# A matrix product by fast multiplication on one core: quarter sums moved between engines, sums of x ahead of weighings, one memory pool per buffer

## The chip, the cores and the metric

The kernel runs on one core of one Trainium2 chip. The metric is device time in microseconds (us), the median of several runs. TensorE (PE) multiplies, VectorE (DVE) and ScalarE (ACT) do element-wise work, GpSimd (POOL) does a little of it, and SyncE (SP) issues nearly all the DMAs. Each engine works through its own queue in order, and waits on semaphores for the others.

## The reference

```python
B, S, D = 8, 2048, 2048          # x: (B, S, D), w: (D, D), float32
cs = np.cumsum(x, axis=1)
diff = cs - np.concatenate([zeros, cs[:, :-1, :]], axis=1)
return np.matmul(diff, w)
```

The difference of a cumulative sum is x itself, so what has to be computed is x @ w: 16384 x 2048 times 2048 x 2048. The kernel does not build the sum.

## The kernel before

**Tiles.** The 16384 rows of x are 128 tiles of 128 rows. Tiles 0 to 3 (`PLAIN = 4`) are multiplied plainly in bf16 while w is still coming in. The other tiles are taken in groups of four, `g, g+1, g+2, g+3`, in float16. A group is two pairs of tiles, (g, g+1) and (h, h+1) with h = g + 2, and each pair is multiplied with w by a scheme of Strassen and Winograd's kind: x and w are split into 2 x 2 blocks, sums and differences of blocks are formed (`S1` to `S4` of x, `T1` to `T4` of w), seven block products are taken instead of eight, and the results are added up. From the second group on some of the seven products are themselves split so, with quarter blocks: `Inner` holds the quarter sums of one block of w (`Q1` to `Q4`, made by `first`, `third` and `fourth`), `sums_in` makes those of x (`one` and `two`, for different blocks `one4`, `two4`, and so on). The first group, `group_plain`, uses block products alone; the second, at g = 8, takes the branch of `group` where `five` is false; the third and all later ones take the other branch.

**One tile of x** goes through these steps: `load` (two DMAs of 512 KB into a buffer of `F`, on SP's queue), `weigh` (ScalarE sums absolute values, half a row at a time), `scale_of` (VectorE makes the row's scale of it, GpSimd the unit `u` with which results are scaled back), `narrow` (ScalarE scales and casts to float16), `turn` (two DMA transposes on SP's queue). `where[t]` says which two buffers of `F` tile t uses: tile 7 (`PLAIN + 3`) uses `F[:, 2]` and `F[:, 3]`. Tile 5 is loaded into the room of `xP`, the plain tiles' x.

**Results** are gathered in float32 tiles `c` of 128 x 512: `keep` copies a PSUM bank into one (ScalarE), `add` adds a bank to it (VectorE), `put` stores it (SP's queue). `keeps`, `adds` and `puts` do this for two.

**Order.** The order on every engine is written by hand. Each instruction goes through a helper that ties it behind the last one of its engine:

```python
def after(engine, ask):
    if engine in last:
        with tc.issue_after(last[engine].ins):
            said = ask()
    ...
```

So the place of a line in the source is its place in that engine's queue. A line of the profile is that of the helper: L515 is the matmul of `product`, L534 that of `quarter`, L545 `add`, L542 `keep`, L505 `total` (sums of x), L502 `less` (differences of w), L357 and L361 `block` (w scaled to float16, by VectorE and ScalarE), L425 the making of `T1`, L112 `weigh`, L129, L131 and L132 `scale_of`, L143 `narrow`, L156 `turn`, L100 `load`, L556 `put`, L260 the store of a plain result, L250 the plain matmul.

**The head** is all up to the first group. When the plain tiles of the second half of w are done (`finish_row`), eight results `done` are stored from tiles of the pools `ring` and `o`, and `left_over` makes the one plain block that had no room. Then those pools are closed and their memory is used by the pools of `c` (`cpool`, on `ring`) and of `inner` (`inpool`, on `o` and on `first`, which holds `xP`). `inner` holds in its parts `S1` of both pairs, the sums in passing (`passing`), quarter sums of w, and in the first group two results. A tile that takes memory of a closed pool waits for the last use of what lay there.

In the first group VectorE's queue between the product of `S1g` and that of `S2h` reads as follows; in the second group GpSimd makes one set of quarter differences:

```python
scale_of(h + 1)                    # first group, h + 1 = 7
less(T2[6:], B22[6:], T1[6:])
...
total(S4g, A12g, S2g, SUB)
less(T3, B22, B12)
scale_of(g + 4)
total(S1h, A21h, A22h, ADD); total(S3h, A11h, A21h, SUB); total(S2h, S1h, A11h, SUB)
```
```python
in_4.first()                       # second group: Q1 and Q2, eight differences on DVE
in_4.third("pool")                 # four on GpSimd
```

Of the kernel before, what the change touches and what calls it, by code (L numbers as in the profile page):

```python
# [10 lines left out]
def kernel(  # L11
# [6 lines left out]
    nc = tc.nc  # L18
    P = 128
# [5 lines left out]
    KH = KO // 2  # L25
    NH = N // 2
# [49 lines left out]
# [4 lines that stand above are left out]
        else:  # L80
            said = ask()
        last[engine] = said[-1] if isinstance(said, tuple) else said
        return said
# [74 lines left out]
                    ),  # L158
                )

    with tc.tile_pool(name="ring", bufs=7) as ring, tc.tile_pool(
        name="o", bufs=5
    ) as opool, tc.tile_pool(name="first", bufs=1) as first:
        xP = first.tile([P, PLAIN, KO, P], bf16, name="xP")
        eye = first.tile([P, P], bf16, name="eye")
        wmax = first.tile([P, 2 * KO], f32, name="wmax")
# [63 lines left out]
        def taken(h, ko):  # L230
            wt = whole[ko % KH][:, ko // KH, h, :]
            i = h * KO + ko
            b = wb[h, ko] = ring.tile([P, NH], bf16, name="wb")
            after("act", lambda: nc.scalar.copy(b, wt))  # L234
            after(
                "dve",
                lambda: nc.vector.tensor_reduce(  # L237
                    wmax[:, i : i + 1], wt, AX.X, MAX, apply_absolute_value=True
                ),
            )  # L240
# [21 lines left out]
        def plain_out(h, r):  # L262
            for n in here(h, r):
                if h == r == 0:
                    c = F[:, 2, ds(n * NB, NB)]
                elif h == 0 or r > 1 or r == 1 and n:
                    c = opool.tile([P, NB], f32, name="o")
                else:
                    c = ring.tile([P, NH], bf16, name="wb").bitcast(f32)
                after("act", lambda: nc.scalar.copy(c, ps[r][n]))  # L270
                done.append((c, ds(r * P, P), ds(h * NH + n * NB, NB)))

# [130 lines left out]
        x5 = there[:, : 2 * K].bitcast(f32)  # L403
        where[PLAIN + 1] = [x5[:, :NH], x5[:, NH:]]
        after("sp", lambda: nc.sync.dma_start(x5, x2[ds((PLAIN + 1) * P, P), :]))
        narrow(PLAIN + 2)
        turn(PLAIN + 2)
        finish_row(2)
# [1 line left out]
            block(B21, 1, 0, k, "dve")  # L410
        weigh(PLAIN + 1)
        finish_row(3)
        for k in range(KH):
            block(B12, 0, 1, k, "dve")
        for c, rows, columns in done:
            after("sp", lambda: put(c, rows, columns, nc.sync))
        scale_of(PLAIN + 1)
        narrow(PLAIN + 1)
        turn(PLAIN + 1)
        left_over(bank(2))  # L420
        load(PLAIN + 3, 0)
        load(PLAIN + 3, 1)

        for k in range(KH):
            after("dve", lambda: nc.vector.tensor_tensor(T1[k], B12[k], B11[k], SUB))  # L425
# [17 lines left out]
            return self.all[:, ds(k * P, P)]  # L443


    cpool = ctx.enter_context(tc.tile_pool(name="C", bufs=1))
    inpool = ctx.enter_context(tc.tile_pool(name="inner", bufs=1))
    spills = ctx.enter_context(
        tc.tile_pool(name="spills", bufs=1, space=bass.MemoryType.DRAM)
    )  # L450
    inner = inpool.tile([P, 24, NB], f16, name="inner")
    flow = inpool.tile([P, 4, NB], f16, name="flow")
    spill = [spills.tile([P, 4, NB], f16, name=f"spill{i}") for i in range(1, 3)]
    spare = [inner[:, j, :] for j in range(8, 24)]
    spare += [B12[k][:, n, :] for k in range(KH) for n in range(2)]
    spare += [B22[k][:, 0, :] for k in range(4, 8)]
    spare.reverse()
    S1 = [Part(inner[:, ds(2 * i, 2), :]) for i in range(2)]
    passing = [Quarter(inner[:, j, :]) for j in range(4, 8)]
    free = [cpool.tile([P, NB], f32, name=f"c{i}") for i in range(7)]  # L460
    free.append(free.pop(0))

    def pair():
        return [one_c() for _ in range(2)]
# [5 lines left out]
    class Inner:  # L470
# [14 lines left out]
                self.Q4 = [spare.pop() for _ in range(4)]  # L485
            less(self.Q4, self.t21, self.Q2)

        def third(self, engine="dve"):
            less(self.t12, self.t22, self.t12, engine)

    passed = [flow[:, k, :] for k in range(4)]

# [3 lines left out]
    def bring_flow(i):  # L496
        after("sp", lambda: nc.sync.dma_start(flow, spill[i - 1]))

    def less(dst, p, q, engine="dve"):
        on = {"dve": nc.vector, "pool": nc.gpsimd}[engine]  # L500
        for k in range(len(dst)):
            after(engine, lambda: on.tensor_tensor(dst[k], p[k], q[k], SUB))  # L502

    def total(dst, p, q, op):
        after("dve", lambda: nc.vector.tensor_tensor(dst.all, p.all, q.all, op))  # L505
# [84 lines left out]
    def group_plain(g, X, Y, Z, V):  # L590
        h = g + 2
        ug, uh, vg = unit[g], unit[h], unit[g + 1]
        A11g, A12g = parts(g)
        A11h, A12h = parts(h)
        A21g, A22g = parts(g + 1)
        A21h, A22h = parts(h + 1)
        S1g, S1h = S1
        S2g, S2h, S3g, S3h, S4g, S4h = A11g, A11h, A21g, A21h, A12g, A12h
        load(g + 4, 0)
        load(g + 4, 1)  # L600
        product(X, A11g, B11, True)
        for k in range(3):
            block(B22, 1, 1, k, "act")
        C11g = pair()
        keeps(C11g, X, ug)
        for k in range(3, KH):
            block(B22, 1, 1, k, "act" if k < 6 else "dve")
        product(V, A12g, B21, True)
        product(Y, A11h, B11, True)
        less(T2[:1], B22[:1], T1[:1])  # L610
        adds(C11g, V, ug)
        puts(C11g, g, 0)
        less(T2[1:2], B22[1:2], T1[1:2])
        total(S1g, A21g, A22g, ADD)
        total(S3g, A11g, A21g, SUB)
        total(S2g, S1g, A11g, SUB)
        less(T2[2:6], B22[2:6], T1[2:6])
        product(Z, A12h, B21, True)
        weigh(h + 1)
        C11h, C22g = (  # L620
            [
                inner[:, ds(j, 2), :].rearrange("p a n -> p (a n)").bitcast(f32)
                for j in (i, i + 2)
            ]
            for i in (16, 20)
        )
        keeps(C11h, Y, uh)
        scale_of(h + 1)
        less(T2[6:], B22[6:], T1[6:])
        vh = unit[h + 1]  # L630
        product(V, S1g, T1, True)
        keeps(C22g, V, vg)
        narrow(h + 1)
        turn(h + 1)
        load(h + 4, 0)
        total(S4g, A12g, S2g, SUB)
        product(X, S2g, T2, False)
        C12g = pair()
        keeps(C12g, X, ug)
        less(T3, B22, B12)  # L640
        product(V, S4g, B22, False)
        weigh(g + 4)
        scale_of(g + 4)
        narrow(g + 4)
        load(h + 4, 1)
        turn(g + 4)
        load(g + 5, 0)
        load(g + 5, 1)
        product(X, S3g, T3, False)
        total(S1h, A21h, A22h, ADD)  # L650
        total(S3h, A11h, A21h, SUB)
        total(S2h, S1h, A11h, SUB)
        adds(C11h, Z, uh)
        puts(C11h, h, 0)
        del free[-2:]
        adds(C12g, V, ug)
        puts(C12g, g, 1)
        product(Y, S2h, T2, False)
        C12h = pair()
        keeps(C12h, Y, uh)  # L660
        adds(C22g, X, vg)
        puts(C22g, g + 1, 1)
        del free[-2:]
        total(S4h, A12h, S2h, SUB)
        product(Z, S1h, T1, True)
        weigh(h + 4)
        less(T4[:4], B21[:4], T2[:4])
        scale_of(h + 4)
        less(T4[4:], B21[4:], T2[4:])
        C22h = pair()  # L670
        keeps(C22h, Z, vh)
        narrow(h + 4)
        weigh(g + 5)
        product(Y, S3h, T3, False)
        in_2.first()
        in_2.fourth()
        load(h + 5, 0)
        load(h + 5, 1)
        turn(h + 4, [0])
        scale_of(g + 5)  # L680
        adds(C22h, Y, vh)
        puts(C22h, h + 1, 1)
        product(Z, S4h, B22, False)
        in_2.third()
        adds(C12h, Z, uh)
        puts(C12h, h, 1)
        narrow(g + 5)
        weigh(h + 5)
        turn(h + 4, [1])
        turn(g + 5, [0])  # L690
        product(X, A22g, T4, False)
        C21 = pair()
        keeps(C21, X, vg)
        puts(C21, g + 1, 0)
        turn(g + 5, [1])
        product(Y, A22h, T4, False)
        less(in_3.Q1, in_3.t12, in_3.t11)
        scale_of(h + 5)
        C21 = pair()
        keeps(C21, Y, vh)  # L700
        narrow(h + 5)
        less(in_3.Q2, in_3.t22, in_3.Q1)
        turn(h + 5)
        load(g + 8, 0)
        load(g + 8, 1)
        puts(C21, h + 1, 0)


    def group(g, X, Y, q, e, v, w):
# [42 lines left out]
        two()  # L752
        if g == PLAIN + 4:
            in_3.fourth()
        if g > PLAIN + 4:
            total(S1g, A21g, A22g, ADD)
            total(S3g, A11g, A21g, SUB)
            total(S2g, S1g, A11g, SUB)
# [159 lines left out]
        else:  # L918
# [16 lines left out]
            keeps(C22g, (v, w), vg)  # L935
            adds(C12g, (v, w), ug)
            puts(C12g, g, 1)
            in_4.first()
            in_4.third("pool")
            product((q, e), S1h, T1, True)  # L940
            C22h = pair()
            keeps(C22h, (q, e), vh)
            adds(C12h, (q, e), uh)
            puts(C12h, h, 1)
            go(P7g, 2)
            one4()
            two4()
            turn(next_k, [0])
            adds(C22g, X, vg)
# [5 lines left out]
            puts(C22h, h + 1, 1)  # L955
            weigh(next_l)
            scale_of(next_l)
            load(then, 1)

        a11, a12, a22, s1, s2, s3, s4 = A4  # L960
# [72 lines left out]
```

## Time and profile before

| what | us |
|---|---|
| median of 3 runs (lowest, highest) | 1489.5 (1489.13, 1490.81) |
| the profiled execution | 1490.04 |
| its span, first to last instruction | 1488.0 |
| TensorE busy in it | 1470.6 (99%) |
| VectorE, ScalarE, GpSimd busy | 1293.4 (87%), 913.8 (61%), 74.5 (5%) |

The granted clock of TensorE was 1.00 throughout. The profiled execution is one more run; what lies around its span is 2.0 us. Times in the timelines are counted from the start of the span. The head ends and the first group begins at 75 us, the second group begins at 125 us, the third at 174 us, and from there on a group takes 45.1 us.

### The profile page before, as it was taken

To read this page: it belongs to the slowest core of one execution; us is meant where nothing else is said; L and a number is where in the kernel's file an instruction comes from. 1 tells how busy PE (TensorE), PEld (TensorE's weight loads), DVE (VectorE), ACT (ScalarE), POOL (GpSimd) and SP (SyncE) were. 2 spreads that over 40 slices of the span, in tenths; PEclk is the share of its full clock that TensorE was granted. 3 is DMA by queue.
4 is the path that set the end of the run, shared out by engine and by line. 5 is a ranking of instruction groups with operands and counts; after the bars stand their busy time and mean duration, and the time that the engine had idled before them with its cause. 6 is when DMAs were issued, how large, how long until landed. Compare 5 with 4: busy or idle time off the path is not lost.

```text
span 1488.0 us, 21123 instructions
## 1 busy us (share of the span) xinstructions
PE 1470.6 (99%) x6789; PEld 663.2 (45%) x6795; DVE 1293.4 (87%) x2430; ACT 913.8 (61%) x1301; POOL 74.5 (5%) x140
## 2 busy tenths in 40 slices
PE   8999999999999999999999999999999999999998
PEld 3444444444444444444444444444444444444443
DVE  7998998888888888888888888888888888888887
ACT  5877566665665655666655666656656556657542
POOL 0110100000000000000000000000000000000000
PEclk9999999999999999999999999999999999999999
DMA  9999799999999999989999989999989999999983
GB/s 363 357 245 285 204 263 266 246 266 269 246 256 247 259 266 267 251 255 238 264 271 258 250 259 243 260 274 245 263 243 259 262 265 256 254 238 266 274 204 129
DMA packets 386255, 382.59 MB, mean 257 GB/s; under 512 B 275744, under 2 KB 275744, under 8 KB 386016
## 3 DMA queue, kind: packets, MB, share of 16 engines
q1 hardware_dynamic: 385584, 379.41, 92.0%
q0 software_dynamic: 560, 1.84, 0.3%
q8 instruction: 53, 0.87, 0.2%
q14 instruction: 58, 0.48, 0.1%
HBM read 180.88 MB, written 135.27 MB: 212 GB/s over the span
## 4 chain that ended last, share of the span: by engine, by line
PE 91%; DMA 3%; DVE 3%; ACT 2%; issue 1%; SPq 0%; DVEq 0%; ACTq 0%
PE b L534 47%; PE b L515 43%; DVE c L545 2%; PE b L250 2%; DMA W<-in_w_dram 2%; DMA F<-in_x_dram 1%; DVE W L502 0%; DMA W<-in_x_dram 0%; DMA out_dram<-wb 0%; ACT F L143 0%; ACT waste L112 0%; ACT wb L234 0%; ACT W L361 0%; ACT o L270 0%; ACT c L542 0%
## 5 line engine op out<-in xcount | busy, mean ns | idle before, releaser
L545 DVE SCALAR_TENSOR_TENSOR c<-b,u,c 128x512 f32<-128x512 f32 x1051 | 746.8, 746 | 153.7 <-PE b L534 85.6
L515 PE MATMUL b<-W,x 128*128 128x512 f16 x3072 | 716.7, 379 | 1.1 <-DVE x L505 1.1
L542 ACT ACTIVATE c<-b,u 128x512 f32<-128x512 f32 x492 | 315.0, 681 | 337.9 <-PE b L534 172.8
L515 PEld LDWEIGHTS <-x 128*128 128x128 f16 x3072 | 300.4, 98 | 364.0 <-DVE x L505 2.0
L143 ACT ACTIVATE F<-F,s 128x1024 f16<-128x1024 f32 x246 | 282.3, 1147 | 110.3 <-DVE s L131 106.3
L534 PE MATMUL b<-W,inner 128*128 128x512 f16 x1416 | 344.1, 379 | 0.0
L112 ACT ACTIVATE waste<-F 128x1024 uint8<-128x1024 f32 x246 | 259.5, 1055 | 99.4 <-DMA F<-in_x_dram 95.4
L534 PEld LDWEIGHTS <-inner 128*128 128x128 f16 x1772 | 173.3, 98 | 209.1
L534 PEld LDWEIGHTS <-x 128*128 128x128 f16 x1560 | 152.3, 98 | 194.2 <-issue 13.4
L534 PE MATMUL b<-W,x 128*128 128x512 f16 x964 | 233.1, 379 | 4.3 <-DVE c L545 2.9
L132 POOL TENSOR_SCALAR u<-m,uw 128x1 f32<-128x1 f32 x124 | 64.1, 522 | 1296.4 <-DVE m L129 1288.7
L505 DVE TENSOR_TENSOR x<-x,x 128x1024 f16<-128x1024 f16 (+1 forms) x214 | 120.4, 574 | 6.1 <-PE b L515 0.7
L534 PE MATMUL b<-flow,x 128*128 128x512 f16 x356 | 91.3, 379 | 0.0
L505 DVE TENSOR_TENSOR inner<-x,x 128x1024 f16<-128x1024 f16 (+1 forms) x122 | 67.5, 553 | 1.8 <-DMA x<-F 1.8
L250 PE MATMUL b<-wb,xP 128*128 128x512 bf16 x234 | 57.0, 394 | 4.8 <-ACT wb L234 3.1
L534 PE MATMUL b<-inner,x 128*128 128x512 f16 x240 | 61.6, 379 | 0.0
L534 PE MATMUL b<-inner 128*128 128x512 f16 x240 | 61.6, 379 | 0.0
L112 ACT ACTIVATION_READ_ACCUMULATOR waste<-F 128x1 f32 x246 | 46.6, 190 | 0.0
L505 DVE TENSOR_TENSOR x<-inner,x 128x1024 f16<-128x1024 f16 x62 | 42.4, 683 | 3.2
L505 DVE TENSOR_TENSOR inner<-inner 128x512 f16<-128x512 f16 x116 | 43.9, 420 | 1.0
L502 DVE TENSOR_TENSOR flow<-W,inner 128x512 f16<-128x512 f16 x120 | 42.6, 418 | 0.0
L237 DVE TENSOR_REDUCE wmax<-W 128x1 f32<-128x1024 f32 x32 | 38.9, 1219 | 3.4 <-DMA W<-in_w_dram 2.0
(57 smaller groups left out, 416.7 us busy)
## 6 DMA issues: line engine op xcount, KB each, us to landing
F<-in_x_dram SPq DMA_DIRECT2D x246, 512.0 KB, 5.2
out_dram<-c SPq DMA_DIRECT2D x492, 256.0 KB, 4.1
flow<-spill SPq DMA_DIRECT2D x57, 512.0 KB, 3.7
W<-in_w_dram SPq DMA_DIRECT2D x32, 512.0 KB, 9.6
W<-in_x_dram SPq DMA_DIRECT2D x16, 256.0 KB, 7.4
x<-F SPq DMA_TRANSPOSE x246, 3.9
out_dram<-o POOLq DMA_DIRECT2D x5, 256.0 KB, 4.0
out_dram<-o SPq DMA_DIRECT2D x5, 256.0 KB, 3.7
```

The source lines that it names most:

```text
L112: lambda: nc.scalar.activation(waste, where[t][i], ABS, scale=1.0 / ROW, accum_out=sums_of[t][:, i : i + 1],),
L132: after("pool", lambda: nc.gpsimd.tensor_scalar(u, m, uw, None, MUL))
L143: lambda: nc.scalar.activation(narrowed(t)[:, ds(i * NH, NH)], where[t][i], COPY, scale=s),
L237: lambda: nc.vector.tensor_reduce(wmax[:, i : i + 1], wt, AX.X, MAX, apply_absolute_value=True),
L250: lambda: nc.tensor.matmul(ps[r][n], xP[:, r, ko, :], wb[h, ko][:, ds(n * NB, NB)], start=(ko == 0), stop=(ko == KO - 1),),
L502: after(engine, lambda: on.tensor_tensor(dst[k], p[k], q[k], SUB))
L505: after("dve", lambda: nc.vector.tensor_tensor(dst.all, p.all, q.all, op))
L515: said = nc.tensor.matmul(to[n], a[k], b[k][:, n, :], start=(first and k == 0), stop=(k == KH - 1), skip_group_check=True,)
L534: said = nc.tensor.matmul(to, a[k], b[k], start=(first and k == 0), stop=(k == 3), skip_group_check=True)
L542: after("act", lambda: nc.scalar.activation(c, p, COPY, scale=u))
L545: after("dve", lambda: nc.vector.scalar_tensor_tensor(c, p, u, c, MUL, ADD))
```

## The change

- **Second group (g = 8).** `in_4.third` is done by VectorE instead of GpSimd and comes later, behind `scale_of(next_l)`; `less` has no engine to choose any more. `in_4.Q1` (half of `in_4.first`) is made at the group's start, behind `in_3.fourth`. `one4` comes ahead of `adds(C12h, (q, e), uh)`.
- **First group (g = 4).** Tile 7 (h + 1) is weighed ahead of three of the conversions `block(B22, ...)` on ScalarE; its `scale_of`, `narrow` and `turn` come directly behind the sums `S1g` to `S2g`, ahead of `T2[2:]` on VectorE and of `keeps(C11h)` and `keeps(C22g)` on ScalarE. The sums `S1h`, `S3h`, `S2h` come ahead of `weigh(g + 4)` and `scale_of(g + 4)` in the source, so ahead of tile 8's scale on VectorE.
- **Loads and stores in the head.** Tile 7 is loaded right behind tile 5, instead of behind the left-over's store. Of the eight stores of plain results two (`done[0]`, `done[3]`) stay ahead of the transposes of tile 5; the other six go behind them.
- **Pools.** Every tile of `ring`, `o` and `C` has a pool of its own (`alone`), and so have `S1g` and `S1h` (no longer parts of `inner`), `inner` (20 columns instead of 24) and `flow`. `turn_of` takes the tiles in turn.

```diff
-    with tc.tile_pool(name="ring", bufs=7) as ring, tc.tile_pool(
-        name="o", bufs=5
-    ) as opool, tc.tile_pool(name="first", bufs=1) as first:
+    def alone(shape, dtype, name, until=ctx):
+        pool = until.enter_context(tc.tile_pool(name=f"{name}_", bufs=1))
+        return pool.tile(shape, dtype, name=name)
+
+    with ExitStack() as head:
+        ring = [alone([P, NH], bf16, f"wb{i}", head) for i in range(7)]
+        results = [alone([P, NB], f32, f"o{i}", head) for i in range(5)]
+        first = head.enter_context(tc.tile_pool(name="first", bufs=1))
+
+        def turn_of(tiles):
+            tiles.append(tiles.pop(0))
+            return tiles[-1]
...
         after("sp", lambda: nc.sync.dma_start(x5, x2[ds((PLAIN + 1) * P, P), :]))
+        load(PLAIN + 3, 0)
+        load(PLAIN + 3, 1)
         narrow(PLAIN + 2)
         turn(PLAIN + 2)
...
-        for k in range(KH):
+        for k in range(5):
             block(B12, 0, 1, k, "dve")
-        for c, rows, columns in done:
-            after("sp", lambda: put(c, rows, columns, nc.sync))
+        for k in range(5, KH):
+            block(B12, 0, 1, k, "dve")
         scale_of(PLAIN + 1)
         narrow(PLAIN + 1)
+        for c, rows, columns in (done[0], done[3]):
+            after("sp", lambda: put(c, rows, columns, nc.sync))
         turn(PLAIN + 1)
+        for c, rows, columns in done[1:3] + done[4:]:
+            after("sp", lambda: put(c, rows, columns, nc.sync))
         left_over(bank(2))
-        load(PLAIN + 3, 0)
-        load(PLAIN + 3, 1)
...
-    cpool = ctx.enter_context(tc.tile_pool(name="C", bufs=1))
-    inpool = ctx.enter_context(tc.tile_pool(name="inner", bufs=1))
+    free = [alone([P, NB], f32, f"c{i}") for i in range(7)]
+    free.append(free.pop(0))
...
-    inner = inpool.tile([P, 24, NB], f16, name="inner")
-    flow = inpool.tile([P, 4, NB], f16, name="flow")
+    S1 = [alone([P, 2, NB], f16, f"S1{i}") for i in range(2)]
+    inner = alone([P, 20, NB], f16, "inner")
+    flow = alone([P, 4, NB], f16, "flow")
...
         keeps(C11g, X, ug)
+        weigh(h + 1)
         for k in range(3, KH):
             block(B22, 1, 1, k, "act" if k < 6 else "dve")
...
         total(S2g, S1g, A11g, SUB)
-        less(T2[2:6], B22[2:6], T1[2:6])
+        scale_of(h + 1)
+        narrow(h + 1)
+        vh = unit[h + 1]
+        turn(h + 1)
+        less(T2[2:], B22[2:], T1[2:])
         product(Z, A12h, B21, True)
-        weigh(h + 1)
...
         keeps(C11h, Y, uh)
-        scale_of(h + 1)
-        less(T2[6:], B22[6:], T1[6:])
-        vh = unit[h + 1]
         product(V, S1g, T1, True)
         keeps(C22g, V, vg)
-        narrow(h + 1)
-        turn(h + 1)
...
         product(V, S4g, B22, False)
+        total(S1h, A21h, A22h, ADD)
+        total(S3h, A11h, A21h, SUB)
+        total(S2h, S1h, A11h, SUB)
         weigh(g + 4)
...
         product(X, S3g, T3, False)
-        total(S1h, A21h, A22h, ADD)
-        total(S3h, A11h, A21h, SUB)
-        total(S2h, S1h, A11h, SUB)
...
         if g == PLAIN + 4:
             in_3.fourth()
+            less(in_4.Q1, in_4.t12, in_4.t11)
...
-            in_4.first()
-            in_4.third("pool")
+            less(in_4.Q2, in_4.t22, in_4.Q1)
             product((q, e), S1h, T1, True)
             C22h = pair()
             keeps(C22h, (q, e), vh)
+            one4()
             adds(C12h, (q, e), uh)
             puts(C12h, h, 1)
             go(P7g, 2)
-            one4()
             two4()
...
             weigh(next_l)
             scale_of(next_l)
+            in_4.third()
             load(then, 1)
```

More of the change, by code (lines that the diff above doesn't have):

```diff
@@ L232, in taken @@
             i = h * KO + ko
-            b = wb[h, ko] = ring.tile([P, NH], bf16, name="wb")
+            b = wb[h, ko] = turn_of(ring)
             after("act", lambda: nc.scalar.copy(b, wt))
@@ L266, in plain_out @@
                 elif h == 0 or r > 1 or r == 1 and n:
-                    c = opool.tile([P, NB], f32, name="o")
+                    c = turn_of(results)
                 else:
-                    c = ring.tile([P, NH], bf16, name="wb").bitcast(f32)
+                    c = turn_of(ring).bitcast(f32)
                 after("act", lambda: nc.scalar.copy(c, ps[r][n]))
@@ L450 @@
     )
-    inner = inpool.tile([P, 24, NB], f16, name="inner")
-    flow = inpool.tile([P, 4, NB], f16, name="flow")
+    S1 = [alone([P, 2, NB], f16, f"S1{i}") for i in range(2)]
+    inner = alone([P, 20, NB], f16, "inner")
+    flow = alone([P, 4, NB], f16, "flow")
     spill = [spills.tile([P, 4, NB], f16, name=f"spill{i}") for i in range(1, 3)]
-    spare = [inner[:, j, :] for j in range(8, 24)]
+    spare = [inner[:, j, :] for j in range(4, 20)]
     spare += [B12[k][:, n, :] for k in range(KH) for n in range(2)]
@@ L457 @@
     spare.reverse()
[L458 to L461, printed above, removed]
+    S1 = [Part(t) for t in S1]
+    passing = [Quarter(inner[:, j, :]) for j in range(4)]
     def pair():
@@ L486, in fourth, with third @@
             less(self.Q4, self.t21, self.Q2)
-        def third(self, engine="dve"):
-            less(self.t12, self.t22, self.t12, engine)
+        def third(self):
+            less(self.t12, self.t22, self.t12)
     passed = [flow[:, k, :] for k in range(4)]
@@ L497, in bring_flow, with less @@
         after("sp", lambda: nc.sync.dma_start(flow, spill[i - 1]))
-    def less(dst, p, q, engine="dve"):
-        on = {"dve": nc.vector, "pool": nc.gpsimd}[engine]
+    def less(dst, p, q):
         for k in range(len(dst)):
-            after(engine, lambda: on.tensor_tensor(dst[k], p[k], q[k], SUB))
+            after("dve", lambda: nc.vector.tensor_tensor(dst[k], p[k], q[k], SUB))
     def total(dst, p, q, op):
@@ L624, in group_plain @@
             ]
-            for i in (16, 20)
+            for i in (12, 16)
         )
         keeps(C11h, Y, uh)
-        scale_of(h + 1)
-        less(T2[6:], B22[6:], T1[6:])
-        vh = unit[h + 1]
         product(V, S1g, T1, True)
         keeps(C22g, V, vg)
-        narrow(h + 1)
-        turn(h + 1)
         load(h + 4, 0)
```

## The prediction

> **What bounds the kernel now.** I read the page first, then the waits of TensorE, then the timelines around each wait. TensorE issues its instructions in the same order before and after, so only its idle time can move.
>
> ```profile
> PE 1470.6 (99%) x6789; PEld 663.2 (45%) x6795; DVE 1293.4 (87%) x2430; ACT 913.8 (61%) x1301; POOL 74.5 (5%) x140
> ```
> ```profile
> PE b L534 <- DVE c L545: 2.9, 3, 1.8
> PE b L515 <- DVE x L505: 1.1, 1, 1.1
> ```
> The second fence is from TensorE's waits: waited for, us in total, times, longest. Past the opening, four waits are all there is, and all are for VectorE. The timelines place them (start, duration, count; idle before in brackets):
>
> ```profile
> 92.42 10.60 PE L515 MATMUL b<-W,x 128*128 128x512 f16 x48
> 104.11 3.63 PE L515 MATMUL b<-W,x 128*128 128x512 f16 x16 [1.09 <-DVE x L505]
> ```
> ```profile
> 159.70 5.34 PE L515 MATMUL b<-W,x 128*128 128x512 f16 x24
> 165.67 1.02 PE L534 MATMUL b<-W,x 128*128 128x512 f16 x4 [0.63 <-DVE c L545]
> 168.52 1.02 PE L534 MATMUL b<-W,x 128*128 128x512 f16 x4 [1.83 <-DVE c L545]
> 169.38 2.75 PE L534 MATMUL b<-W,inner 128*128 128x512 f16 x12
> 171.97 1.03 PE L534 MATMUL b<-flow,x 128*128 128x512 f16 x4
> 173.49 1.04 PE L534 MATMUL b<-W,x 128*128 128x512 f16 x4 [0.49 <-DVE c L545]
> ```
> The bracket undercounts: a matmul's record lasts 0.379 us, but the next is issued after (5.34 - 0.38)/23 = 0.216. From issue to issue, 92.42 + 48 x 0.216 = 102.78 against 104.11: 1.33 lost (**stall A**). 159.70 + 24 x 0.216 = 164.88 against 165.67: 0.79. A quarter of four takes 0.863: 165.67 + 0.86 = 166.53 against 168.52: 1.99; 171.97 + 0.86 = 172.83 against 173.49: 0.66. **Stall B** is these three, 3.44. Together 4.77. Groups from the third on repeat every 45.1 us, with one gap of 0.21 each; the change leaves their order alone on every engine.
>
> **Why VectorE is late at B.**
>
> ```profile
> 158.36 3.34 DVE L502 TENSOR_TENSOR W<-W 128x512 f16<-128x512 f16 x4
> 161.62 3.33 DVE L502 TENSOR_TENSOR W<-W,W 128x512 f16<-128x512 f16 x4
> 169.05 0.41 DVE L502 TENSOR_TENSOR flow<-W 128x512 f16<-128x512 f16 x1
> 169.38 1.09 DVE L502 TENSOR_TENSOR flow<-W,W 128x512 f16<-128x512 f16 x3
> ```
> ```profile
> 158.92 5.09 POOL L502 TENSOR_TENSOR W<-W,W 128x512 f16<-128x512 f16 x4 [4.13 <-DVE W L502]
> ```
> Four such differences take 1.42 us where GpSimd rests (169.05 to 170.47), 3.34 and 3.33 beside `in_4.third("pool")`: 3.8 us of delay, just ahead of the additions that free TensorE's banks.
>
> **The change at B.** I keep before's clock and move VectorE's work in the new order. The additions `adds(C12g, ...)` end at 158.45, as now. `in_4.Q2` alone, 1.42: to 159.8. `one4`, now ahead (0.94 for the same two at 166.20): to 160.65. `adds(C12h, ...)` read a bank that ScalarE reads until 161.06, and end at 162.0 (1.40). `two4` 0.76: 162.7. `adds(C22g, X)` 1.40: 164.1. `fourth` 1.42: 165.4. `adds(C22h, Y)` 1.40, after their matmuls at 165.04: 166.7. `scale_of` 0.4: 167.1. `third`, the four differences from GpSimd, 1.42: 168.5. The addition that empties `X[0]` 0.67: 169.1.
>
> TensorE without stalls starts its seven quarters at 164.88, 165.74, 166.61, 167.47, 168.33, 169.20 and 170.06. The first needs the first half of `adds(C12h)` (161.3, not 165.62), the second that of `adds(C22g)` (163.4, not 168.47), the sixth `fourth` and `adds(C22h)` (165.4 and 166.1). The seventh (`s3`) needs an addition that waits for the fifth to end, 168.33 + 0.65 + 0.38 = 169.36; VectorE is there at 169.1, so it takes 169.40 to 170.15 and the quarter starts 0.06 later: 0.14 to 0.21 remain, the upper value being the gap of every later group at this place. So the four differences added here cost nothing while 0.3 us of room holds; without it each us late is a us of stall. B falls from 3.44 to 0.2.
>
> `in_4.Q1` (1.42) goes to 128.87, ahead of `S1g`, which waits until 130.1 for a transposed tile, after which VectorE waits another 2.08 for TensorE (timeline). Q1 ends at 130.3 and moves `S1g` by 0.2, inside that second wait: nothing. Without this cover it would cost up to 1.4.
>
> **The change at A.** The wait is for `S2h`, the third sum of x (104.06). It stands behind `T3` (to 100.70) and `scale_of(8)`, which waits until 101.47 for ScalarE's weighing of tile 8. That stands behind tile 7's weighing, which had to wait for its load:
>
> ```profile
> 85.61 3.23 ACT L361 ACTIVATE W<-W,uinv 128x1024 f16<-128x1024 f32 x3
> 90.84 1.06 ACT L112 ACTIVATE waste<-F 128x1024 uint8<-128x1024 f32 x1 [2.00 <-DMA F<-in_x_dram]
> 92.42 1.06 ACT L112 ACTIVATE waste<-F 128x1024 uint8<-128x1024 f32 x1 [0.43 <-DMA F<-in_x_dram]
> ```
> The load of tile 7 was issued at 84.90 on SP's queue, behind eight stores, the transposes of tile 5 and the left-over's store. Now it follows tile 5's load (68.44), at 68.8 and 69.3; its buffers are free by 65.9. Tile 5's 1 MB landed at 73.65, and queued halves land 1.3 to 1.5 apart (the four issued from 84.90: 90.82, 92.34, 93.63, 94.89), so tile 7 is there at about 76.3. Queued behind it: tile 6's transposes (landed 75.06 and 76.27, needed at 82.2 and 85.6; 3 us of delay fits), and stores that nobody awaits before 87.1. If the loads shared the bandwidth evenly instead, tile 5 would land 2.2 us later, and the last bank copy, queued behind its weighing on ScalarE, would end at 79.2 where TensorE wants it at 79.0: 0 to 0.3 us. I take 0, since the queued loads landed in order.
>
> On ScalarE tile 7's weighing (2.33) now runs at 85.6, without waiting; the three conversions behind it end at 91.1 instead of 88.84, narrowing at 93.3, `keeps(C11h)` at 94.5, `keeps(C22g)` at 95.6, needed from 96.04: room 0.4. On VectorE: `S1g` to `S2g` as before until 89.24, `scale_of(7)` 89.6, `T2[2:]` 93.2 (the conversions hold back single steps, but TensorE asks only from 93.7), `S4g` 93.8, `T3` 98.6. Tile 7's transposes, at 92.2 and 93.5 instead of 96.95 and 98.24, land (3.2 later) by 96.7. `S1h`, `S3h`, `S2h` take 2.2 with their latencies: 100.8, needed at 102.8. `scale_of(8)` behind them waits for nobody. Stall A goes whole: 1.33.
>
> `turn(5)` ahead of six stores is issued as soon as narrowing ends (79.7 instead of 81.1); the first store of a `c` starts 0.3 later. One pool per buffer removes waits that had ended already: `S1g` waited for eleven stores, the last landed at 84.07, and it started at 87.10 behind VectorE's own work. Both nothing; so is the split `range(5)`, which leaves the order as it was.
>
> **One rule weighed.** When GpSimd's tiny `u` product (L132) runs beside differences, the trace shows VectorE unharmed: at 153.96 it took 0.83 us beside four differences that took 0.42 each, and:
>
> ```profile
> 93.99 1.36 POOL L132 TENSOR_SCALAR u<-m,uw 128x1 f32<-128x1 f32 x1 [14.22 <-DVE m L129]
> 94.01 1.27 DVE L502 TENSOR_TENSOR W<-W 128x1024 f16<-128x1024 f16 x2
> ```
> After the change such a product starts beside `third`; I add nothing for it. The Trainium skill's page "SBUF — State Buffer", section "Who interferes with whom", says that a VectorE instruction with two SBUF inputs and a GpSimd instruction that reads SBUF exclude each other for the whole instruction, whoever issues first; the big GpSimd block agrees, the tiny products do not, and by that rule `third` could be blocked by one: the first rival's time.
>
> **Sum.** The profiled execution took 1490.04 (span 1488.0, 2.0 around it). 1490.04 - 1.33 - 3.44 + 0.2 = 1485.5. It lies 0.5 over the median of the three runs, so the forecast is 1489.5 - 4.6 = **1484.9**. Bounds of the unknowns: 0.3 for tile 5's load, 0.1 less at `s3`.
>
> **Rivals.**
> - VectorE loses the longest `u` product near B, 0.83 us, in `third`: it is at the `s3` addition at 169.95, 0.55 late. 1485.5. For: the slow rows beside GpSimd's four. Against: the two rows above. Chance 0.08.
> - A comes back: tile 7's transposes land at 101.9 instead of 96.7 (what they lose beyond 100.6 is a stall, up to 1.33). 1486.3. Against: 4 us to spare. Chance 0.06.
> - The differences are slow for their operands, not for GpSimd: two of Q2's stay at 1.38, VectorE reaches the `s3` addition at 171.0, 1.6 us late, 1486.5. Against: 1.42 for four of the same shapes everywhere else. Chance 0.04.
> - Slower: tile 7's weighing, now ahead of ScalarE's conversions and keeps, blocks that in-order queue until the second half of its load lands, at T. `keeps(C22g)` then ends 8.8 later (1.16 + 3.13 + 2.33 + 2.40, less 0.2 of overlap), where its second half is wanted at 96.26, so the loss is T - 87.4. No gain is left from T = 92.0; T = 94.9, where the last of the four queued loads landed, gives 1492.4; from T = 95.0 it is slower by over 0.2%. For: the order of that queue is fixed. Against: 18 us of delay for a load issued at 68.8. Chance 0.04.
>
> Something that no row shows has 0.06, with 1487 to 1489. The forecast keeps 0.72.
>
> **Range and chances.** 0.2% is 3.0 us, about what a measurement of this kernel tells from no change. From 1484.1 (half the spread of the runs, 0.8, under the forecast) to 1487.0 (0.5 over the third rival) lie the forecast and the first three rivals, 0.90, less what scatter takes. Faster: the forecast, the first rival and about a third of the next two, 0.83. Slower 0.04. Same 0.13.
>
> **What would show it.** Right: no wait of TensorE at the sum of x near 103; the third group starting near 169.8 instead of 174.36; differences of 0.42 us and no L502 on POOL; tile 7's weighing at 85.6 without idle time. Wrong: ScalarE idle at L112 before 91, the `s3` quarter waiting over 0.3 us, or a gap in the third group that the later ones do not have.

## The result and the profile after

| | before | after |
|---|---|---|
| median, same chip (lowest, highest) | 1489.5 (1488.82, 1490.81) | 1485.35 (1484.85, 1485.96) |
| ratio, 95% interval | | 0.997 (0.9959 to 0.9982) |
| profiled execution, its span | 1490.04, 1488.0 | 1485.96, 1484.2 |

The kernel became 4.15 us faster, 0.28%; 4.6 was forecast. The line of TensorE's busy time, from the page of the changed kernel, says as little as before:

```profile
PE 1470.2 (99%) x6795; PEld 663.3 (45%) x6795; DVE 1290.2 (87%) x2434; ACT 914.3 (62%) x1301; POOL 69.5 (5%) x136
```

TensorE's waits, again us in total, times, longest, now hold only lines of the opening (plain matmuls L260, transposes L223, the matmuls on zeros L287 that stand ahead of all others). Both lines that carried the prediction are gone:

```profile
PE b L260 <- ACT wb L244: 3.7, 6, 1.9
PE b L287 <- DVE xP L186: 1.2, 1, 1.2
...
```

Stall A, timeline of TensorE (start, duration): the 64 matmuls run through to the sum of x without a gap where there was one behind the 48th.

```profile
93.24 13.98 PE L527 MATMUL b<-W,x 128*128 128x512 f16 x64
107.05 3.62 PE L527 MATMUL b<-W,S 128*128 128x512 f16 x16
```

The reason, timeline of ScalarE: tile 7's weighing (L112) follows the keeps of `C11g` without idle time, and the conversions (L371) come behind it.

```profile
85.29 1.25 ACT L554 ACTIVATE c<-b,u 128x512 f32<-128x512 f32 x2
86.43 1.05 ACT L112 ACTIVATE waste<-F 128x1024 uint8<-128x1024 f32 x1
87.61 1.06 ACT L112 ACTIVATE waste<-F 128x1024 uint8<-128x1024 f32 x1
88.67 3.21 ACT L371 ACTIVATE W<-W,uinv 128x1024 f16<-128x1024 f32 x3
```

Stall B, TensorE's seven quarters: 0.863 apart but for the last, 168.67 to 169.74, where 0.21 are lost.

```profile
159.17 5.34 PE L527 MATMUL b<-W,x 128*128 128x512 f16 x24
164.35 1.89 PE L546 MATMUL b<-W,x 128*128 128x512 f16 x8
166.08 1.03 PE L546 MATMUL b<-W,S 128*128 128x512 f16 x4
...
168.67 1.03 PE L546 MATMUL b<-flow,x 128*128 128x512 f16 x4
169.74 1.02 PE L546 MATMUL b<-W,x 128*128 128x512 f16 x4
```

And VectorE: `Q2` at 157.84 and `third` at 166.32 take 1.42 and 1.41 for four differences; after one addition, VectorE is idle for 0.55 us until TensorE's fifth quarter is done. GpSimd's one tiny product lies beside `third`.

```profile
157.84 1.42 DVE L514 TENSOR_TENSOR W<-W,W 128x512 f16<-128x512 f16 x4
166.32 1.41 DVE L514 TENSOR_TENSOR W<-W,W 128x512 f16<-128x512 f16 x4
168.94 3.71 DVE L557 SCALAR_TENSOR_TENSOR c<-b,u,c 128x512 f32<-128x512 f32 x5 [0.55 <-PE b L546]
```
```profile
166.30 0.83 POOL L132 TENSOR_SCALAR u<-m,uw 128x1 f32<-128x1 f32 x1 [12.04 <-DVE m L129]
```

### The profile page after: what moved, and what is told of

It reads as the page before. It is cut to its first block, busy times and chain, and to the rows that moved or that the text cites. A ratio compares the mean times of both kernels' runs of the same rounds, so it can differ in the third digit from the quotient of the medians.

```text
span 1484.2 us, 21118 instructions
## 1 busy us (share of the span) xinstructions
PE 1470.2 (99%) x6795; PEld 663.3 (45%) x6795; DVE 1290.2 (87%) x2434; ACT 914.3 (62%) x1301; POOL 69.5 (5%) x136
## 4 chain that ended last, share of the span: by engine, by line
PE 94%; DMA 2%; DVE 2%; ACT 0%; issue 0%; SPq 0%; DVEq 0%; ACTq 0%
PE b L546 46%; PE b L527 45%; PE b L260 2%; DVE c L557 2%; DMA W<-in_w_dram 2%; DMA W<-in_x_dram 0%; DMA out_dram<-c 0%; ACT wb L244 0%; PE b L385 0%; ACT o L280 0%; ACT c L554 0%; SPq L204 0%; DVEq L1040 0%; DVEq L557 0%; SPq L238 0%
## 5 line engine op out<-in xcount | busy, mean ns | idle before, releaser
L112 ACT ACTIVATE waste<-F 128x1024 uint8<-128x1024 f32 x246 | 259.5, 1055 | 95.3 <-DMA F<-in_x_dram 91.2
L546 PE MATMUL b<-W,inner 128*128 128x512 f16 x828 | 212.5, 379 | 0.0
L546 PEld LDWEIGHTS <-inner 128*128 128x128 f16 x1068 | 104.5, 98 | 126.0
L546 PE MATMUL b<-W,S 128*128 128x512 f16 x588 | 146.2, 379 | 0.0
L546 PEld LDWEIGHTS <-S 128*128 128x128 f16 x704 | 68.9, 98 | 83.1
L260 PE MATMUL b<-wb,xP 128*128 128x512 bf16 x240 | 57.4, 393 | 5.1 <-ACT wb L244 3.7
L112 ACT ACTIVATION_READ_ACCUMULATOR waste<-F 128x1 f32 x246 | 46.6, 189 | 0.0
L517 DVE TENSOR_TENSOR x<-S,x 128x1024 f16<-128x1024 f16 x62 | 42.3, 683 | 3.2
L517 DVE TENSOR_TENSOR S<-x,x 128x1024 f16<-128x1024 f16 x62 | 42.2, 681 | 0.0
```

The lines of the kernel that those rows point to most:

```text
L112: lambda: nc.scalar.activation(waste, where[t][i], ABS, scale=1.0 / ROW, accum_out=sums_of[t][:, i : i + 1],),
L260: lambda: nc.tensor.matmul(ps[r][n], xP[:, r, ko, :], wb[h, ko][:, ds(n * NB, NB)], start=(ko == 0), stop=(ko == KO - 1),),
L546: said = nc.tensor.matmul(to, a[k], b[k], start=(first and k == 0), stop=(k == 3), skip_group_check=True)
```

## Where the time goes, execution by execution

The traces are cut at the first weight load of each group's first product. The opening varies from one execution to the next, whatever the kernel; behind it a stretch without a varying stall repeats to a few hundredths, so the stretches show what single times hide. One profiled execution each, us:

| kernel | first group starts at | first group | second | third |
|---|---|---|---|---|
| before | 74.94 | 49.69 | 49.52 | 45.39 |
| before_1, before_2 | 75.83, 74.83 | 49.02, 48.65 | 50.57, 50.73 | 45.32, 45.32 |
| after | 75.76 | 48.35 | 46.29 | 45.31 |
| only_b | 74.69 | 48.86 | 46.29 | 45.32 |
| engine_only | 75.09 | 48.35 | 47.02 | 45.32 |
| only_a | 74.68 | 48.35 | 49.52 | 45.74 |
| sums_only | 75.31 | 48.60 | 50.15 | 45.49 |
| sums_back | 75.58 | 48.35 | 46.29 | 45.31 |
| late_load | 75.39 | 55.27 | 46.28 | 45.31 |
| old_pools | 75.25 | 49.94 | 46.29 | 45.32 |
| q1_late | 75.33 | 48.35 | 47.00 | 45.31 |
| pool_late | 76.20 | 48.35 | 47.00 | 45.31 |
| swap | 75.36 | 48.35 | 46.08 | 45.11 |

What follows the third group, up to the end of the last matmul, took 1263.0 in all but the last (1257.3).

The opening's variation arises early: in all fourteen traces the last 127 weight loads ahead of the first group take 27.41 us, so the difference is there before 49 us, ahead of the early load of tile 7 (69.69 in the changed kernel).

## The experiments

Each ran beside the kernel before on the same chip, whose median was 1489.6 to 1490.6 there.

**only_b.** The kernel before with the second group's edits (the last three of the diff above).

> The kernel before with the second group's part alone: the four differences of third moved from GpSimd to VectorE behind scale_of(next_l), Q1 to the group's start, one4 ahead of adds(C12h). The theory has two independent stalls, A (1.33 us, the third sum of x behind tile 8's scale) and B (3.44 us, VectorE's differences slowed beside GpSimd's). Expected: A stays at 1.25 to 1.33, B's three gaps go but for 0.14 to 0.21 at the s3 quarter, time 3.2 us under the kernel before, 1486.3. Rival: VectorE's delay at B came in part from the later head, so that without it one of B's gaps stays: 1487 to 1488.

Measured 1486.19, ratio 0.9976 (0.9967 to 0.9985). The second group is that of the changed kernel, 46.29: part B stands alone, and the rival falls. But stall A was 0.51 in this execution, not 1.25, with the head of the kernel before. The sum had taken it from one execution.

**only_a.** The changed kernel with these three edits undone.

> The changed kernel with the second group's part undone (third on GpSimd in its old place, Q1 and one4 in theirs); head, first group and pools as changed. Expected by the theory: no wait of TensorE near 103, the differences beside GpSimd at 3.3 us for four again and B's three gaps back at 0.8, 2.0 and 0.65; time 1.3 us under the kernel before, 1488.2. Rival: the head brings nothing by itself, since what it gains is lost again in front of the second group's wait: 1489.5.

Measured 1489.28, ratio 0.9997 (0.9988 to 1.0006). The median lies 1.28 us under that of before (1490.56), as expected, but the ratio gives 0.4 us and its interval holds 1: by the times inconclusive. The trace has the first group of the changed kernel (48.35) and B's gaps as before. In the third group TensorE waits 0.42 us more for VectorE (45.74 us for the group), so a part of what A gives is lost again there. VectorE's differences are slow again in their old place:

```profile
156.76 3.34 DVE L515 TENSOR_TENSOR W<-W 128x512 f16<-128x512 f16 x4
160.02 3.34 DVE L515 TENSOR_TENSOR W<-W,W 128x512 f16<-128x512 f16 x4
```

**engine_only.** One word of the kernel before:

```diff
             in_4.first()
-            in_4.third("pool")
+            in_4.third()
```

> The kernel before with one word changed: third of in_4 runs on VectorE in its old place, directly behind in_4.first, and nothing is moved. VectorE does 1.42 us more there, and the differences should go from 6.7 us to 2.8 (theory: GpSimd beside them slowed them). Walked with the rows of before: adds(C12h) end at 163.9 instead of 166.3, the first gap goes, the second falls from 1.99 to 0.5, the third stays at 0.7; 2.2 us of B's 3.44 go, time 2.2 us under the kernel before. Rival: the place, not the engine, makes VectorE late, and 1.42 us more of work make the gaps longer: slower than before by up to 1.4.

Measured 1486.59, ratio 0.9975 (0.9965 to 0.9985): by the medians 3.9 us under before, where 2.2 were expected. The twelve differences in a row take 4.1 us on VectorE, where eight beside GpSimd took 6.6:

```profile
157.18 1.42 DVE L502 TENSOR_TENSOR W<-W 128x512 f16<-128x512 f16 x4
158.51 2.77 DVE L502 TENSOR_TENSOR W<-W,W 128x512 f16<-128x512 f16 x8
```

The second group is 2.50 shorter than in the first profile of before, the gaps left are 0.29 and 0.65. So the engine, not the place, is the larger part; Q1, `one4` and `third` in their new places bring the other 0.73 (47.02 to 46.29). The other 1.4 us of the 3.9 are not assigned: this execution had no stall A, and before sometimes loses clock as well (before_1 below).

**pool_late.** The changed kernel with `in_4.third("pool")` in the new place.

> The changed kernel with third of in_4 on GpSimd in its new place, behind scale_of(next_l). VectorE then has only additions beside it, with one input in SBUF and one in PSUM. Theory: what collides is the reading of two SBUF inputs, so the additions keep 0.75 us; GpSimd starts at about 167 and takes up to 1.27 us for each difference (5.09 for four before), the last ends near 172.2 and the s3 quarter, wanted from 169.5 on, waits about 2 us: 1487.3 (1485.5 if GpSimd alone needs no more than 0.6 us each). Rival: any work of VectorE collides, the additions take over 1 us each and the waits pile up: over 1488.

Measured 1486.14, ratio 0.9972 (0.9961 to 0.9983), a gap of 0.69 more than in the changed kernel.

```profile
167.00 4.50 POOL L515 TENSOR_TENSOR W<-W,W 128x512 f16<-128x512 f16 x4
```
```profile
169.39 2.20 DVE L558 SCALAR_TENSOR_TENSOR c<-b,u,c 128x512 f32<-128x512 f32 x3 [1.84 <-PE b L547]
```

GpSimd takes 1.12 us for each difference beside additions (1.27 beside differences, before), and three additions beside it take 2.20, as anywhere. This agrees with the theory: differences with two SBUF inputs collide with GpSimd's, additions that read SBUF and PSUM do not. (The additions also differ in operation and type; no run separates that from where the inputs lie.) The 2 us were too much because GpSimd was faster than bounded and only the last matmul of the quarter waited.

**q1_late.** The changed kernel with `in_4.first()` in the old place instead of Q1 early and Q2 there.

> The changed kernel with Q1 of in_4 made in its old place, directly ahead of Q2, so that VectorE has 1.42 us more between the additions of C12g and the s3 quarter; third stays on VectorE. The prediction gave that chain 0.3 us of room (the trace of the changed kernel shows 0.55 us of idle time ahead of the addition that frees the bank). Expected: the gap at s3 grows by 0.9 us, from 0.21 to 1.1, time 1486.3. Rival: VectorE catches up in another idle time and nothing moves, 1485.4.

Measured 1486.37, ratio 0.9971 (0.9963 to 0.998). The gap at `s3` grows from 0.21 to 0.92, the second group from 46.29 to 47.00: 0.7 of 1.42 is a stall, the rest was idle time. TensorE's line of that quarter:

```profile
170.03 1.02 PE L546 MATMUL b<-W,x 128*128 128x512 f16 x4 [0.75 <-DVE c L557]
```

**sums_only and sums_back.** The first is the kernel before with the three `total` lines of h ahead of `weigh(g + 4)`, the second the changed kernel with them behind `product(X, S3g, T3, False)` again.

> The kernel before with one edit: the sums S1h, S3h and S2h ahead of tile 8's scale_of. VectorE reaches them at 100.7 instead of 101.8, but tile 7's second transpose landed at 101.43, so the third sum is done at 103.7 instead of 104.06. Expected: 0.4 us of stall A's 1.33 go, 1489.1. Rival: the order of the sums is the whole of it, 1488.2.

> The changed kernel with the sums S1h, S3h and S2h behind tile 8's scale_of again. In the changed kernel that scale waits for nobody (ScalarE's weighing of tile 8 ended at 100.2, VectorE came at 101.4), so it costs 0.4 us of VectorE's time and the third sum is done at 102.0, where TensorE asks at 103.6. Expected: nothing, 1485.4; the early load of tile 7 is what removed stall A. Rival: the sums' new order removed it, and 1.3 us come back: 1486.7.

sums_back: 1485.41, ratio 0.9974 (0.9964 to 0.9985), first group 48.35, no stall: the sums' new order is not needed for A. What is left there is the early load together with the earlier weighing and turning of tile 7; no run has the load alone. sums_only: 1489.94, ratio 1.0004 (0.9995 to 1.0013), nothing to be told by time; its stall A was 0.25. Its second group was 0.6 longer than in the first profile of before; the cause of these small gaps stays open.

**late_load.** The changed kernel with tile 7 loaded in the old place:

```diff
         after("sp", lambda: nc.sync.dma_start(x5, x2[ds((PLAIN + 1) * P, P), :]))
-        load(PLAIN + 3, 0)
-        load(PLAIN + 3, 1)
...
         left_over(bank(2))
+        load(PLAIN + 3, 0)
+        load(PLAIN + 3, 1)
```

> The changed kernel with tile 7 loaded behind the left-over's store again, as before, while its weighing stays ahead of ScalarE's three conversions and its keeps: the slower rival of the prediction, made real. The load is issued at about 87.5 in the changed kernel's time, and its second half lands at 94 to 95 (T). By the rival's sum (T - 87.4, and 0.8 less because this profile's opening ended 0.8 later) 5.8 to 6.8 us are lost: 1491 to 1492. If ScalarE's queue is no bound there: 1485.4, and 1.33 more if only the third sum of x comes late again: 1486.7.

Measured 1491.91, ratio 1.0017 (1.0009 to 1.0026): the slower rival exists, at its price. The second half landed at 94.75; with this execution's opening (0.45 later) the sum gives 94.75 - 87.4 - 0.45 = 6.9, and the first group is 6.92 longer. ScalarE stood still for it (7.05 us ahead of the first half, 0.47 ahead of the second), and TensorE's first wait was for `T2`, behind ScalarE's conversions, only the second for the keeps that the rival named. TensorE's waits between 80 and 110:

```profile
PE b L527 <- DVE W L514: 3.6, 2, 3.2
PE b L527 <- ACT inner L554: 0.9, 1, 0.9
```
```profile
93.21 1.06 ACT L112 ACTIVATE waste<-F 128x1024 uint8<-128x1024 f32 x1 [7.05 <-DMA F<-in_x_dram]
```

**old_pools.** The changed kernel with the pools of before (the pool edits of the diff undone).

> The changed kernel with the pools of before: one pool each for ring, o, C and inner, S1 inside inner. The prediction gave the pools nothing by themselves. With the new order of stores they should matter: S1g then waits for all the stores of o, the last landed at 89.96 in the changed kernel, so it starts 2 us later than 87.92 and is done at 90.7, where TensorE asks for it at 89.8; the first keep of C11g waits for the stores of ring, 86.8 instead of 85.3. Expected: a gap of 0.9 us (0.6 to 1.3) at the product of S1g, time 1486.3. Rival: the waits are covered as in the kernel before, 1485.4.

Measured 1486.92, ratio 0.9981 (0.9972 to 0.999), the gap at the product of `S1g` 1.60, more than the 0.9 expected (0.6 to 1.3). VectorE's sum waits for a store of `o` and ends at 90.66; TensorE's product of it starts at 90.87:

```profile
89.97 0.69 DVE L508 TENSOR_TENSOR inner<-x,x 128x1024 f16<-128x1024 f16 x1 [0.58 <-DMA out_dram<-o]
```

So with the new order of stores the new pools are needed. No run has them with the old order, and none undoes the order of the stores alone.

**before_1 and before_2.** The kernel before, unchanged.

> The kernel before, another execution: how large is stall A in it, and where does the first group begin. The sum took 1.33 from one execution. In the kernel that has only the second group's part, whose head is the same as before, it was 0.50, and the second half of tile 7 landed 16.6 us behind the first group's start instead of 17.4. If stall A follows that landing, each us of landing is a us of stall. If the 0.50 came from the change instead, A is 1.25 again here.

> The kernel before once more, for the same question: the spread of stall A and of the opening from one execution to the next. Expected: stall A between 0.4 and 1.4, following the landing of tile 7; the first group's start anywhere from 74.6 to 75.8 as in all kernels; B's three gaps at 0.79, 1.99 and 0.65 as ever.

1491.25 and 1490.06, one run each. Stall A was 0.67 and 0.30, so it varies. Put beside the landing of tile 7's second half, counted from the first group's start, five executions with the old head give

| landing | 17.40 | 16.73 | 16.58 | 16.36 | 15.42 |
|---|---|---|---|---|---|
| stall A (first group less 48.35) | 1.34 | 0.67 | 0.51 | 0.30 | 0.00 |
| kernel | before | before_1 | only_b | before_2 | engine_only |

that is, the landing less 16.06, to 0.01, and nothing for a landing before that. (sums_only landed at 16.68 and lost 0.25 instead of 0.62: its edit is worth the 0.4 expected.) B's first two gaps were as ever (0.80 and 1.99), but the second group was longer by 1.05 and 1.21. That is a lower clock behind the longest gap. In before_1 the quarter behind it is issued at half the pace:

```profile
168.75 1.86 PE L534 MATMUL b<-W,x 128*128 128x512 f16 x4 [1.83 <-DVE c L545]
170.41 3.43 PE L534 MATMUL b<-W,inner 128*128 128x512 f16 x12
```

and the stretches of that trace show the granted clock (the column behind the engines' busy times) at 0.59 and 0.56 (over 168.35 to 171.76 alone it is 0.50; the next stretch has 1.00 again), where the first profile of before, in the last line, has 1.00:

```profile
168.00:170.00 2.00, 1.25 (x4) 0.42 (x4) 2.00 (x6) 0.00 (x0) 0.00 (x0) 0.59 1.00 232
170.00:172.00 2.00, 2.00 (x7) 0.77 (x6) 2.00 (x6) 0.00 (x0) 0.00 (x0) 0.56 0.76 288
```
```profile
168.00:170.00 2.00, 1.48 (x7) 0.68 (x7) 2.00 (x5) 0.00 (x0) 0.00 (x0) 1.00 1.02 245
```

It happened in two of the five traces with B's gaps. The third gap shrinks meanwhile, from 0.66 to 0.22, since VectorE catches up, so 1.1 to 1.2 of the loss remain.

The timed runs show how often. The lost clock lowers a run's mean granted clock to 0.998, as in these two. Of the 71 runs of before beside the experiments 23 list 0.998, and on each chip they are 0.5 to 1.2 us longer in the mean than the others there. Of only_a and sums_only, which keep B's long gap, 4 of 11 each do; of the 68 runs of the changed kernel, only_b, engine_only, old_pools, q1_late, sums_back, pool_late and swap, which do not have it, none does.

**swap.** The changed kernel with two quarters exchanged in the last section of every group:

```diff
-        quarter(X[1], s4, Q.t22, False)
+        quarter(q, s2, Q.Q2, False)
         turn(next_k, [1])
         turn(next_l, [0])
-        quarter(q, s2, Q.Q2, False)
+        quarter(X[1], s4, Q.t22, False)
```

> The changed kernel with two quarters exchanged in the last section of every group: q(s2) ahead of X[1](s4). The gap of 0.21 us that each group has at the s3 quarter is read as the time in which VectorE empties q (0.04 to begin, 0.75 to add, 0.06 until TensorE goes on) less the one quarter of 0.86 between the two uses of q, with a little lateness. With two quarters between them it should vanish in all 30 groups that have it: 30 x 0.21 = 6.3 us, time 1479.0. Rival: the gap is not that wait, or VectorE and ScalarE come late for the quarter put ahead: no gain, 1485.4 or more.

Measured 1479.13, ratio 0.9932 (0.992 to 0.9945): 6.2 under the changed kernel, the best version here. The 0.21 at `s3` is gone in every group. In the third group the last two quarters start 0.87 apart, where in the changed kernel they start at 213.77 and 214.84, 1.07 apart:

```profile
213.16 1.03 PE L546 MATMUL b<-flow,x 128*128 128x512 f16 x4
214.03 1.03 PE L546 MATMUL b<-W,x 128*128 128x512 f16 x4
```

The sum of the expectation (0.04 + 0.75 + 0.06 less 0.86) does not itself give 0.21. The rows of the changed kernel's second group do: the fifth quarter's last record ends at 168.83, the addition runs from 168.94 to 169.69, and TensorE goes on at 169.74, 0.91 in all. Without a wait it would have gone on at 168.67 + 0.863 = 169.53, 0.70 behind that record's end, so 0.21 are lost.

## Why the prediction was right, and where its sizes were off

- **B, right in mechanism and size.** Forecast 3.44 less 0.2; the second group went from 49.52 to 46.29, 3.23. engine_only and pool_late show that it was GpSimd's block beside two-input differences. The room at `s3` was 0.55 us rather than 0.3; of the 1.42 us that q1_late puts ahead of it, 0.71 became a stall. What the sum did not know is that the long gap sometimes costs TensorE's clock too, 1.1 to 1.2 more, in about a third of the runs of before.
- **A, right in mechanism, mis-sized as a usual value.** The term "1.33" is what one execution lost. It is the lateness of one landing, 0 to 1.34 in five executions, 0.56 in the mean. What is certain is that it goes: 48.35 in every kernel with the early load and the new pools. The walk counted both the load and the sums' order; sums_back shows that the sums' order is not needed, sums_only that the order alone brings 0.4; the rest of the wait is for tile 7's own transposes, which the late load delays as well (in sums_only VectorE's sums wait 0.78 us for them).
- **The sum.** From trace to trace the groups went down by 1.34 + 3.23 + 0.08 = 4.65 against 4.57 forecast, while the two profiled executions differ by 4.08: the opening was 0.82 longer in that of the changed kernel. The opening's spread over all traces, 74.7 to 76.2, is larger than the miss of 0.45 in the median. The traces of before give A and B together, the clock included, 4.57, 4.95 and 4.74. An estimate for the timed runs from these rows: 0.56 for A in the mean, 3.23 for B and a third of 1.1 to 1.2 for the clock make 4.2, near the measured 4.15. So the closeness of 4.6 is in part luck: the forecast's A was about 0.8 too large as a usual value, and a clock loss of about 0.4 that it left out made up half of that. The split of the timed runs themselves is not measured.
- **What was costed at nothing.** Q1's new place and tile 6's delayed transposes (landed at 79.04 and 81.40, 3.2 and 4.3 behind the old ones measured from the groups' start, still in time) were free. Tile 5's load, priced at 0 to 0.3, landed 1.43 ahead of the first group's start, where it was 1.29 before: not delayed. The pools were put at nothing against the old order of the stores; with the new order the old pools cost 1.6 us (old_pools).
- **The rivals.** The first (GpSimd's `u` product blocks `third`) is out: 166.30 to 167.13 beside four differences that took 1.41. By the rule of the Trainium skill's page "SBUF — State Buffer", section "Who interferes with whom", they should exclude each other. The prediction read the tiny products as against it, since VectorE was unharmed; but it is GpSimd that waits. The product takes 0.28 us alone or beside additions, and 0.58 to 1.36 beside VectorE's sums and differences; the 0.83 that this rival charged to VectorE was mostly GpSimd's own waiting. A coming back and slow operands are out by the trace after. The slower rival was real but needed the late load.

## What to carry to other kernels

Before a wait in one profile is booked as a gain, look at what it waits for: if the chain begins at a DMA's landing, its size is that execution's, and a second trace is worth more than a third digit. Moving a small job to an idle engine is only free if the busy engine does not run into it: compare the same instruction's time beside and away from the other engine. And a gap of 0.21 us that stands in every group (30 of them here) is worth more than the three of 3.44 together that the wait list names.

## What the runs showed of the hardware

- TensorE's granted clock was 0.50 for 3.4 us behind a gap of 2 us (before_1 from 168.35 to 171.76, and before_2), and likewise in late_load behind one of 3.4. The first profile, with the same gaps, kept 1.00. The Trainium skill's page "TensorE: Matmul & The Clock Gate", section "The HAM clock gate", puts the fall behind an idle window of about 3.4 us. In before_1 and before_2 less was enough, a gap of 0.8 and one of 2.0 with four matmuls between them, and the measurement decides.
- Differences of 128x512 in float16 on VectorE and GpSimd take turns. Of VectorE's eight in the first profile of before, the four that met a GpSimd difference took 1.37 to 1.38 us each, as in the line below, and the other four 0.41 to 0.42. GpSimd's four took 5.09 us there and 4.50 beside additions. So each of the four lost 0.95 us, nearly the 1.12 that a GpSimd difference lasts, and GpSimd lost 0.15 on each of its own.

```profile
159.03 1.38 DVE L502 TENSOR_TENSOR W<-W 128x512 f16<-128x512 f16 x1
```
- The tiny `u` product is held up in the same way, by VectorE. In the trace of the changed kernel it took 0.28 to 0.29 us in the 59 cases beside additions or alone (as in pool_late, below), and 0.58 to 1.36 in the 63 beside VectorE's sums and differences, which read two SBUF inputs. The longer these are, the longer the product: it took 0.83 beside differences of 128x512 (0.42 each) and 1.36 beside those of 128x1024 (0.67 and 0.68), and ended 0.07 us behind the second of them both times.

```profile
166.76 0.28 POOL L132 TENSOR_SCALAR u<-m,uw 128x1 f32<-128x1 f32 x1 [12.05 <-DVE m L129]
```
